# A search stage replanned: other costs and a port in the planner, low parts moved from GpSimd to VectorE, and the last two dense blocks of a chunk interleaved

## The chip, the cores and the metric

The kernel runs on one core of a Trainium2 chip. The metric is the device time of one execution in microseconds (us); the time given for a kernel is the median of several executions. Beside the times there is one execution recorded by the hardware profiler, and all rows below are from it. PE is TensorE (matmuls), PEld its weight loads, DVE is VectorE, ACT is ScalarE, POOL is GpSimd, SP is the engine that issues most DMAs.

## The reference, cut to what matters

One layer of a gated block on 4096 tokens of width 1024. The input is normalised and multiplied by one wide matrix; its columns become a sparse attention, a pooling branch and several gates.

```python
h = rms_norm(x, norm_g)
proj = h @ w_in
q, k, v, qi, ki, wi, z_a, u_b, z_b, gates = jnp.split(proj, SPLIT_POINTS, axis=-1)
...
logits = jnp.einsum('bqhd,bsd->bqhs', qib, ki)              # 8 index heads, width 32
iscore = jnp.einsum('bqhs,bqh->bqs', jax.nn.relu(logits), wib)
iscore = jnp.where(allowed[None], iscore, -jnp.inf)         # chunks of 64 keys
_, idx = lax.top_k(iscore, k_sel)                           # the best 256 keys of each query
...
outs.append((c - lagged) / count - ug[:, :, g])             # trailing means over 2, 4, 8, 16
mixed = jnp.einsum('bsgc,gcd->bsgd', pooled, pool_w)
b = mixed * pool_scale * silu(z_b)
g = sigmoid(gates + merge_bias)
y = g[:, :, 0] * (a @ w_branch_a) + g[:, :, 1] * (b @ w_branch_b)
x = x + y @ w_out
```

The search is the part from `logits` to `idx`: each query of a block of 128 needs the 256 best of all keys allowed to it. The dense projections are the columns `z_a`, `u_b`, `z_b` and `gates` of `h @ w_in`.

## The kernel before, in words

The work runs in stages. Phase 1 normalises x, computes the columns for attention and search, and writes the normalised input, transposed and split in a high and a low part, to DRAM. The index stage (`phase_index`, with `dense` in it) does the search for query blocks 2 to 31 and, beside it, the dense projections. Then come attention, the two branch products and the output product. Only the index stage is touched by the change.

**Split matmuls.** Products are computed as high x high + high x low + low x high. A weight tile is loaded (`wraw`), its high part `wgh` is a copy on ACT (L1157), and its low part `wgl` is the difference of the two, on POOL (L1158). Four of the 28 weight tiles are split earlier, in phase 1, on DVE (L697).

**Search.** For each block b there are 128(b+1) keys, in pieces of 1024. POOL fills the score tile with a tie-break by `iota` (L882). For each of 8 heads PE multiplies into one of two score banks `ps` (L894), ACT takes the Relu into one of four `rl` tiles (L897), and DVE multiplies by the head's weight and adds (L899, two SBUF inputs). The score tiles share one large tile, `ring`. Blocks form 18 groups, the large ones alone. For each group a threshold is found in seven rounds: ACT counts the scores over it by a Sign with a sum (L984), and some 20 small DVE instructions update it (`update`, L943 to L972). `finish` takes the largest of the rest (L1012, L1013), decides (L1020 to L1024, the last writes `flag`), and writes a bias row `bt` (L1032), which goes to DRAM.

**Dense.** Six sweeps of 5 or 4 channel tiles (blocks) go over 8 chunks of 512 tokens: 28 x 8 = 224 blocks. A chunk's h tiles (8 of them, 512 KB each) are loaded into a ring of 12. A block is 8 steps over the channel tiles k; a step is three matmuls of 512 columns into one of three banks `pd` (L1188 to L1190), and needs the pair of h tiles that holds channel tiles k and k+1. All steps stand in one chain. A finished block is read by ACT and DVE (`gate`, L1132 to L1139), or, for the first two blocks of four of the sweeps, by `pool`: ACT copies it (L1096, L1097), POOL adds shifted copies (`sums`, L1106), DVE takes the mean (L1115), ACT and POOL split it (L1117, L1118), PE multiplies it by the pool matrix (L393 to L395), and DVE scales it (L1122).

**What sets the order.** Nothing is scheduled on the chip: each engine runs its queue in the order in which the program was written, and waits at an instruction until its inputs and its tile are ready. That order comes from a planner, `Plan`. Each `pl.add` gives a step its engine, an estimated cost in us, a key, and the steps it follows. `Plan.run` simulates the engines: a free engine takes the ready step with the lowest key whose tiles are free in their rings, and the step's instructions are written out then. A dependent on another engine becomes ready 0.1 us (`LAT`) later, one on a DMA 2 us later. Search steps have keys from 12 to 1042, spread by a formula in `span`; a dense step's key is its place times `unit`; what follows a dense block has a very low key and so goes first.

```python
m = pl.add("pe", n * 0.42e-3, k_, mm, have + [base[o]] + ..., use=[ps, t])
r = pl.add("act", 0.05 + n * 0.834e-3, k_, ...activation(rl, ps, AF.Relu), [m], use=[ps, rl])
prev[o] = pl.add("dve", 0.1 + n * 1.04e-3, k_, ...scalar_tensor_tensor(acc, rl, wi, acc), [r, prev[o]], use=[rl])
...
prev = pl.add("pe", 5.0 / KT, t, mm, [l0, l1, have, prev], use=[pd, wh, wl, h0, h1])
t += unit / KT
```

Of the kernel before, what the change touches and what calls it, by code (L numbers as in the profile page):

```python
# [12 lines left out]
F32 = mybir.dt.float32  # L13
# [37 lines left out]
LAT = 0.1  # L51
# [73 lines left out]
class Step:  # L125
    def __init__(self, eng, cost, key, fn, after, use, form):
        self.eng, self.cost, self.key, self.fn, self.use, self.form = eng, cost, key, fn, use, form
        self.wait, self.then, self.ready = 0, [], 0.0
        for x in after:
            self.wait += 1  # L130
            x.then.append(self)
        for x in self.use:
            x.users += 1


class Plan:
# [11 lines left out]
    def new(self, name, role=None):  # L148
        return Tile_(name, role)
# [25 lines left out]
    def add(self, eng, cost, key, fn, after=(), new=(), use=(), form=0):  # L175
        s = Step(eng, cost, key, fn, [x for x in after if x is not None], (*new, *use), form)
        self.steps.append(s)
        return s

    def run(self, lat):  # L180
        ready = {}
        busy = {}
        form = {}
        now, order, done, left = 0.0, 0, [], len(self.steps)
        seq = {id(s): i for i, s in enumerate(self.steps)}

        def push(s):
            insort(ready.setdefault(s.eng, []), (s.key, seq[id(s)], s.ready))

        for s in self.steps:  # L190
            if not s.wait:
                push(s)
        while left:
            start, nxt = None, None
            for eng, q in ready.items():
                free = busy.get(eng, 0.0)
                if free > now:
                    nxt = free if nxt is None else min(nxt, free)
                    continue
                for i, (_, n, t) in enumerate(q):  # L200
                    if t > now:
                        nxt = t if nxt is None else min(nxt, t)
                        continue
                    s = self.steps[n]
                    if self.room(s.use):
                        start = (q, i, s)
                        break
                if start:
                    break
            if start:  # L210
                q, i, s = start
                del q[i]
                for x in s.use:
                    if x.t is None:
                        p = self.place(x.ring)
                        self.rings[x.ring][p] = x
                        x.t = self.make[x.ring](p)
                s.fn()
                s.end = busy[s.eng] = now + s.cost + (CHF if form.get(s.eng, 0) != s.form else 0.0)
                form[s.eng] = s.form  # L220
                heappush(done, (busy[s.eng], seq[id(s)]))
                continue
            if done and (nxt is None or done[0][0] <= nxt):
                now, n = heappop(done)
                s = self.steps[n]
                left -= 1
                for x in s.use:
                    x.users -= 1
                    if not x.users:
                        order += 1  # L230
                        x.freed = order
                for d in s.then:
                    d.wait -= 1
                    d.ready = max(d.ready, now + (2.0 if s.eng == "dma" else lat if d.eng != s.eng else 0.0))
# [20 lines left out]
class K:  # L255
# [520 lines left out]
    def phase_index(self):  # L776
# [92 lines left out]
        def scores(b, key, total, free):  # L869
# [6 lines left out]
            while os_:  # L876
# [3 lines left out]
                for o in some:  # L880
                    n = min(1024, L - o)
                    prev[o] = base[o] = pl.add("pool", 0.1 + n * 1.65e-3, key(0) - 3, lambda o=o, n=n: po.iota(  # L882
                        acc[:, o:o + n].bitcast(I32), pattern=[[1, n]], base=-(2 ** 31) + (27 << 23) + 1 + o,
                        channel_multiplier=0), free)
                for h in range(8):
                    for o in some:
# [4 lines left out]
                        def mm(ps=ps, o=o, n=n, h=h):  # L891
# [3 lines left out]
                        m = pl.add("pe", n * 0.42e-3, k_, mm, have + [base[o]] + kd[:max(0, (o + n - S) // P + 2)],  # L895
# [3 lines left out]
                        prev[o] = pl.add("dve", 0.1 + n * 1.04e-3, k_, lambda rl=rl, o=o, n=n, h=h: v.scalar_tensor_tensor(  # L899
                            acc[:, o:o + n], rl.t[:, :n], self.wi[:, b, h:h + 1], acc[:, o:o + n], op0=OP.mult,  # L900
                            op1=OP.add), [r, prev[o]], use=[rl])
# [3 lines left out]
        def topk(gi, key, scored):  # L905
# [68 lines left out]
            last = pl.add("dve", 1.0, key, start, [guessed], use=[tk])  # L974
            done = []
            for i in range(7):
# [13 lines left out]
                if i < 6:  # L990
                    last = pl.add("dve", 1.6 if i < 2 else 2.1, key, lambda i=i: update(i), ev, use=[tk])
            return done

        def finish(b, j, key, sg, tk, evals):
# [10 lines left out]
            s0 = pl.add("dve", 0.4, key, begin, evals, use=[tk, v9])  # L1005
            for p in range(n_p):
# [7 lines left out]
                pieces.append(pl.add("dve", 0.3 + n * 2.08e-3, key, best, [s0], use=[sg, z, v9, cand]))  # L1014
# [10 lines left out]
            s1 = pl.add("dve", 1.0, key, choose, pieces, use=[v9, cand, tk, sel, j9])  # L1025
            flags.append(s1)
            out = []
            for p in range(n_p):
# [3 lines left out]
                s = pl.add("dve", 0.08 + n * 0.52e-3, key, lambda bt=bt, o=o, n=n: v.tensor_scalar(  # L1032
# [33 lines left out]
        pl.run(LAT)  # L1066
# [5 lines left out]
    def dense(self, pl, new, rp):  # L1072
# [16 lines left out]
        def pool(c, g, t, pu, pz, done):  # L1089
# [11 lines left out]
            def sums():  # L1101
# [6 lines left out]
                if c == 0:  # L1108
                    po.tensor_tensor(cur[:, 16:32], cur[:, 16:32], self.cst[:, 32 + 16 * g:48 + 16 * g], op=OP.mult)
            s = chain[g] = pl.add("pool", 0.2 + 1.25 * (g + 1), k, sums, [e0, e1], use=[u, x0] + ([x1] if g else []))  # L1110
# [5 lines left out]
                cur.t[:, 16:], cur.t[:, 16:], 1.0 / win, u.t[:, 16:], op0=OP.mult, op1=OP.subtract), [s], use=[cur, u])  # L1116
# [3 lines left out]
            s = pl.add("pe", 0.62, k, lambda: self.mm3(pm.t, lambda k: wm[g][0], lambda k: wm[g][1],  # L1120
# [26 lines left out]
        def weight(s, m, kind, i, t):  # L1147
# [3 lines left out]
            def load():  # L1151
                o = 0
                for c0, w in cols[kind](i):
# [4 lines left out]
            l = pl.add("pool", 2.3, t - WSP, lambda: po.tensor_tensor(lo.t, raw.t, hi.t.bitcast(F32), op=OP.subtract),  # L1158
                       [h], use=[raw, hi, lo])
# [3 lines left out]
        unit = 5.04  # L1163
        prev = None
        for s, mine in enumerate(sweeps):
# [3 lines left out]
            for c in range(NCH):  # L1169
# [9 lines left out]
                for m, (kind, i) in enumerate(mine):  # L1179
                    pd = new("pd")  # L1180
                    wh, wl, have = W[s, m]
                    for k in range(KT):
                        (h0, l0), (h1, l1) = H[k // 2 * 2:k // 2 * 2 + 2]

                        def mm(k=k, pd=pd, wh=wh, wl=wl, h0=h0, h1=h1):
                            out = pd.t.rearrange("p (r n) -> p r n", n=P)
                            r1, r2 = h0.t[:, :, k % 2], h1.t[:, :, k % 2]
                            pe.matmul(out, wh.t[:, k], r1, start=(k == 0), stop=False)  # L1188
                            pe.matmul(out, wh.t[:, k], r2, start=False, stop=False)  # L1189
                            pe.matmul(out, wl.t[:, k], r1, start=False, stop=(k == KT - 1))  # L1190
                        prev = pl.add("pe", 5.0 / KT, t, mm, [l0, l1, have, prev], use=[pd, wh, wl, h0, h1])
                        t += unit / KT
# [1019 lines left out]
```

## Time and profile before

| | |
|---|---|
| median of 3 executions | 4097.2 us (4094.45 to 4098.45) |
| the profiled execution | 4089.81 us, its span 4088.1 us |
| PE / DVE / ACT / POOL busy in the span | 97% / 80% / 55% / 49% |
| mean granted TensorE clock | 0.990 |
| index stage | 418 to 2032 us |

A group of instructions is read as: line, engine, operation, out<-in by tile names, shapes, count | busy us, mean ns of one | idle time of the engine just before them, and what ended it. A matmul's record is longer than the distance to the next one. A row of waits gives the engine and line that waited, what released it, and the total, the number and the longest of the waits.

### The profile page before, as it was taken

The page shows a single profiled execution, that of the slowest core. Times are in us where ns is not written, and L with a number is a line of the kernel's source. Part 1 is how long each engine was busy: PE and PEld are TensorE (multiplying, and loading weights), DVE is VectorE, ACT ScalarE, POOL GpSimd, SP SyncE. Part 2 cuts the span into 40 slices and gives each one's busy share as a digit, 9 for nine tenths or more (in the row PEclk, how much of TensorE's full clock was granted, in tenths as well). Part 3 has the DMA queues.
Part 4 walks back from the last instruction along what each step waited for, and adds up shares of the span by engine and source line. Part 5 has one row for each costly group of instructions (what it writes and reads, how often), then busy time and mean ns, then how long its engine had stood idle before and what let it go on. Part 6 is the DMA issues. An engine that isn't in the chain of part 4 may idle for free. (4 is left out here: it accounts for less than half of the span.)

```text
span 4088.1 us, 63978 instructions
## 1 busy us (share of the span) xinstructions
PE 3964.7 (97%) x22958; PEld 3028.6 (74%) x22959; DVE 3255.0 (80%) x6399; ACT 2259.6 (55%) x3165; POOL 2021.8 (49%) x1616
## 2 busy tenths in 40 slices
PE   9999999999999999999889999999999999999999
PEld 8999887777777777888766666666666667887787
DVE  7555788888889888778689999999999995556654
ACT  5444787777767877877445555555454552111221
POOL 4554312122123223010028899999999994334653
PEclk9999999999999999999979999999999999999999
DMA  8877545445444455566554433333222215887543
GB/s 278 277 251 249 180 175 185 148 170 189 168 164 164 167 178 188 203 235 227 197 127 73 87 66 69 61 61 59 46 55 44 47 35 179 268 265 241 177 160 123
DMA packets 515986, 637.36 MB, mean 156 GB/s; under 512 B 230608, under 2 KB 365392, under 8 KB 511696
## 3 DMA queue, kind: packets, MB, share of 16 engines
q1 hardware_dynamic: 490576, 610.03, 47.4%
q10 hardware_dynamic: 25088, 23.21, 2.6%
q8 instruction: 181, 2.97, 0.3%
q14 instruction: 141, 1.16, 0.1%
HBM read 409.48 MB, written 191.76 MB: 147 GB/s over the span
## 5 line engine op out<-in xcount | busy, mean ns | idle before, releaser
L1656 POOL TENSOR_TENSOR acc<-acc,tt 128x1024 f32<-128x1024 f32 x388 | 927.6, 2391 | 62.2 <-ACT tt L1637 35.0
L1637 ACT ACTIVATE tt<-tt 128x1024 f32<-128x1024 f32 (+1 forms) x544 | 561.1, 1034 | 544.3 <-DVE tt L1638 513.5
L1189 PE MATMUL pd<-h,wgh 128*128 128x512 f32 x1792 | 705.6, 394 | 11.3 <-DMA h<-hD 11.2
L1188 PE MATMUL pd<-h,wgh 128*128 128x512 f32 x1792 | 710.8, 397 | 0.2 <-DMA h<-hD 0.2
L899 DVE SCALAR_TENSOR_TENSOR ring<-rl,wi,ring 128x1024 f32<-128x1024 f32 (+7 forms) x624 | 699.1, 1165 | 11.6 <-ACT rl L897 8.4
L1190 PE MATMUL pd<-h,wgl 128*128 128x512 f32 x1792 | 704.1, 393 | 0.0
L897 ACT ACTIVATE rl<-ps 128x1024 f32<-128x1024 f32 (+7 forms) x624 | 536.2, 887 | 184.7 <-DVE ring L899 67.5
L1638 DVE TENSOR_TENSOR tt<-st,bT 128x1024 f32<-128x1024 f32 (+1 forms) x504 | 600.5, 1193 | 12.0 <-PE st L1625 11.9
L984 ACT ACTIVATE sg<-ring,tk 128x2048 fp8e4<-128x2048 f32 (+9 forms) x322 | 485.2, 1508 | 63.8 <-DVE tk L972 34.1
L1677 PE MATMUL pv<-tt,vv 128*64 128x256 f32 x4224 | 515.2, 385 | 1.8 <-ACT ov L1698 1.4
L1566 DVE CUSTOM_DVE_ANT_1 jk<-ps,bias,mf 128x1024 bf16<-128x1024 f32 (+3 forms) x408 | 469.5, 1151 | 16.1 <-PE ps L1557 14.3
L1677 PEld LDWEIGHTS pv<-tt,vv 128*64 128x64 f32 x4224 | 285.6, 137 | 169.1 <-issue 34.8
L1189 PEld LDWEIGHTS pd<-h,wgh 128*128 128x128 f32 x1792 | 338.1, 189 | 85.3 <-DMA h<-hD 18.0
L1190 PEld LDWEIGHTS pd<-h,wgl 128*128 128x128 f32 x1792 | 337.6, 188 | 75.3
L1188 PEld LDWEIGHTS pd<-h,wgh 128*128 128x128 f32 x1792 | 337.7, 188 | 73.9 <-DMA h<-hD 0.6
L894 PE MATMUL ps<-kis,qT 128*128 128x512 f32 (+3 forms) x1136 | 344.1, 388 | 41.1 <-ACT rl L897 40.7
L1981 PE MATMUL p<-g,w 128*128 128x512 f32 x1488 | 345.5, 394 | 1.7 <-DVE g L1904 1.7
L1981 PEld LDWEIGHTS p<-g,w 128*128 128x128 f32 x1488 | 279.3, 188 | 67.7 <-DVE g L1904 2.1
L2130 PE MATMUL p<-w,g 128*128 128x512 f32 x1344 | 314.0, 396 | 3.8 <-DVE g L2109 2.1
L2130 PEld LDWEIGHTS p<-w,g 128*128 128x128 f32 x1344 | 253.5, 189 | 64.2 <-DVE g L2109 2.6
L1557 PE MATMUL ps<-kh,qh 64*128 64x512 f32 (+3 forms) x1320 | 264.6, 418 | 29.7 <-DVE mf L1566 26.8
L894 PEld LDWEIGHTS ps<-kis,qT 128*128 128x128 f32 x1136 | 206.8, 189 | 116.8 <-ACT rl L897 76.3
(360 smaller groups left out, 6737.4 us busy)
## 6 DMA issues: line engine op xcount, KB each, us to landing
h<-hD SPq DMA_DIRECT2D x384, 512.0 KB
g<-gD SPq DMA_DIRECT2D x80, 512.0 KB
hlD<-rhl SPq DMA_DIRECT2D x31, 1216.0 KB
gD<-sgm SPq DMA_DIRECT2D x128, 256.0 KB
q<-hlD SPq DMA_DIRECT2D x61, 512.0 KB
x<-x SPq DMA_DIRECT2D x32, 512.0 KB
hD<-hh SPq DMA_DIRECT2D x32, 512.0 KB
hD<-hl SPq DMA_DIRECT2D x32, 512.0 KB
```

Source lines behind the costliest of these rows:

```text
L894: pe.matmul(ps.t[:, s:e], t.t[:, h], self.kis[:, o + s:o + e], start=True, stop=True)
L897: r = pl.add("act", 0.05 + n * 0.834e-3, k_, lambda ps=ps, rl=rl, n=n: act.activation(rl.t[:, :n], ps.t[:, :n], AF.Relu), [m], use=[ps, rl])
L899: prev[o] = pl.add("dve", 0.1 + n * 1.04e-3, k_, lambda rl=rl, o=o, n=n, h=h: v.scalar_tensor_tensor(acc[:, o:o + n], rl.t[:, :n], self.wi ...
L1188: pe.matmul(out, wh.t[:, k], r1, start=(k == 0), stop=False)
L1189: pe.matmul(out, wh.t[:, k], r2, start=False, stop=False)
L1190: pe.matmul(out, wl.t[:, k], r1, start=False, stop=(k == KT - 1))
L1637: act.activation(tt.t[:, 0:n], tt.t[:, 0:n], AF.Exp)
L1638: ad = last_ve[0] = pl.add("dve", 0.07 + 0.54 * n, key, lambda: v.tensor_tensor(tt.t[:, 0:n], s.t[:, 0:n], bc(bt.t[:, 2 * p:2 * p + n, Non ...
L1656: gp.tensor_tensor(acc.t, first, tt.t, op=OP.add)
L1677: pe.matmul(pv.t[64 * f:64 * f + 64], vv[:, k, 64 * g:64 * g + 64], T[u, p].t[:, k % 2, 2 * f:2 * f + 2], start=(k == 0), stop=(k == b))
L1981: pe.matmul(p.t, blk[i].t[:, k, ms], two(x[k // 2][j].t, F32R)[:, k % 2], start=(k == i == j == 0), stop=(k == 3 and i == 1))
L2130: pe.matmul(p.t, quarter(Q.t, x, F32R)[:, k], blk[y].t[:, k], start=(fresh and k == x == y == 0), stop=(k == 3 and x == 1), skip_group_che ...
```

## The change

The planner: a step can have a number of parts that need the shared port (`port`). Such a step keeps its engine busy; its parts queue for one port, first come first served, DVE's and POOL's together. A DMA step is done, for its tiles and its dependents, `land` us after its cost; the index stage runs with 0.15 us between engines and 2.0 for `land`. The other stages call `run` as before.

```diff
+    def run(self, lat, land=0.0):
...
+                if s.port:
+                    busy[s.eng] = math.inf
+                    heappush(done, (now, seq[id(s)], s.port))
+                    continue
...
-                heappush(done, (busy[s.eng], seq[id(s)]))
+                heappush(done, (busy[s.eng] + (land if s.eng == "dma" else 0.0), seq[id(s)], 0))
...
+                if part:
+                    if part > 0:
+                        line.append((n, part))
+                    if line and shared <= now:
+                        n, part = line.pop(0)
+                        s = self.steps[n]
+                        shared = now + s.cost / s.port
+                        heappush(done, (shared, n, -1))
+                        heappush(done, (shared, n, part - 1))
+                        if part == 1:
+                            s.end = busy[s.eng] = shared
+                    continue
...
-        pl.run(LAT)
+        pl.run(0.15, 2.0)
```

The costs in the index stage (n is the piece's columns):

| step | before | after |
|---|---|---|
| iota, POOL | 0.1 + 1.65 n/1000 | 0.1 + 0.82 n/1000 |
| score matmuls, PE | 0.42 n/1000 | 0.452 n/1000 |
| score step, DVE | 0.1 + 1.04 n/1000 | 0.13 + 1.04 n/1000, port 1 |
| threshold start, DVE | 1.0 | 0.43, port 4 |
| update, DVE, rounds 0 and 1 / later | 1.6 / 2.1 | 1.75 / 2.18 |
| finish begin / best / choose, DVE | 0.4 / 0.3 + 2.08 n/1000 / 1.0 | 0.1 / the same, port 2 / 0.8, port 4 |
| bias row, DVE | 0.08 + 0.52 n/1000 | 0.13 + 0.52 n/1000 |
| sums, POOL, by group | 0.2 + 1.25 (g+1) | 1.45, 2.4, 3.7, 6.0, port g+2 |
| pooled mean, DVE | 0.67 | 0.67, port 1 |
| pool matmuls, PE | 0.62 | 0.68 |
| dense step, PE | 5.0/8 | 5.47/8 |

The program itself: two subtractions go from POOL to DVE, `unit` goes from 5.04 to 5.48, and the last two blocks of each chunk take turns by pairs of channel tiles.

```diff
-            s = pl.add("pool", 1.25, k, lambda: po.tensor_tensor(pq.t, cur.t[:, 16:], ph.t.bitcast(F32), op=OP.subtract),
-                       [s], use=[cur, ph, pq])
+            s = pl.add("dve", 0.6, k, lambda: v.tensor_tensor(pq.t, cur.t[:, 16:], ph.t.bitcast(F32), op=OP.subtract),
+                       [s], use=[cur, ph, pq], port=1)
...
-            l = pl.add("pool", 2.3, t - WSP, lambda: po.tensor_tensor(lo.t, raw.t, hi.t.bitcast(F32), op=OP.subtract),
-                       [h], use=[raw, hi, lo])
+            l = pl.add("dve", 1.19, t - WSP, lambda: v.tensor_tensor(lo.t, raw.t, hi.t.bitcast(F32), op=OP.subtract),
+                       [h], use=[raw, hi, lo], port=1)
...
-        unit = 5.04
+        unit = 5.48
...
-                for m, (kind, i) in enumerate(mine):
-                    pd = new("pd")
+                pds = [new("pd") for _ in mine]
+                todo = [(m, k) for m in range(len(mine) - 2) for k in range(KT)]
+                todo += [(m, k) for k0 in range(0, KT, 2) for m in (len(mine) - 2, len(mine) - 1) for k in (k0, k0 + 1)]
+                for m, k in todo:
+                    kind, i = mine[m]
+                    pd = pds[m]
...
-                        prev = pl.add("pe", 5.0 / KT, t, mm, [l0, l1, have, prev], use=[pd, wh, wl, h0, h1])
-                        t += unit / KT
+                    prev = pl.add("pe", 5.47 / KT, t, mm, [l0, l1, have, prev], use=[pd, wh, wl, h0, h1])
+                    t += unit / KT
+                    if k < KT - 1:
+                        continue
```

## Rows read from the trace of the kernel before

**Rows 1.** The page's first part: the span, and each engine's busy time, share of the span and instructions.
```profile
span 4088.1 us, 63978 instructions
...
PE 3964.7 (97%) x22958; PEld 3028.6 (74%) x22959; DVE 3255.0 (80%) x6399; ACT 2259.6 (55%) x3165; POOL 2021.8 (49%) x1616
```
**Rows 2.** The windows of the index stage, from its first dense matmul to its last: start:end, length, then busy time (and instructions) of PE, PEld, DVE, ACT and POOL, the granted clock, the share of the DMA engines and GB/s.
```profile
418.30:800.00 381.70, 371.91 (x1632) 299.03 (x1630) 311.16 (x775) 297.64 (x355) 84.33 (x92) 0.99 0.50 175
800.00:1400.00 600.00, 576.04 (x2507) 458.47 (x2507) 526.66 (x1377) 452.32 (x583) 157.53 (x142) 0.99 0.48 169
1400.00:1900.00 500.00, 484.77 (x2174) 387.72 (x2173) 394.97 (x1003) 397.44 (x545) 78.19 (x66) 1.00 0.59 201
1900.00:2032.50 132.50, 126.89 (x549) 101.14 (x547) 90.59 (x377) 75.94 (x150) 1.13 (x2) 0.99 0.59 203
sum 1614.20, PE 1559.61 PEld 1246.36 DVE 1323.38 ACT 1223.34 POOL 321.18; mean PE 389.90 PEld 311.59 DVE 330.84 ACT 305.83 POOL 80.29
```
**Rows 3.** The dense line L1188 over the stage (durations in ns: least/median/most, first and last start), and PE's timeline at the end of the stage: start, length, line, operation.
```profile
L1188 PE MATMUL pd<-h,wgh x1792: 387/389/628, 418.4 to 2031.7; 128*128 128x512 f32 x200
...
2032.12 0.40 PE L1190 MATMUL pd<-h,wgl 128*128 128x512 f32 x1
2034.13 0.85 PE L387 MATMUL st<-identr,k 128*128 128x128 f32 x8 [1.61 <-DVE zsm L1134]
```
**Rows 4.** PE's timeline in a stretch of dense matmuls only: the first and the 52nd of it, 51 issues apart.
```profile
2000.04 0.39 PE L1188 MATMUL pd<-h,wgh 128*128 128x512 f32 x1
...
2011.70 0.40 PE L1188 MATMUL pd<-h,wgh 128*128 128x512 f32 x1
```
**Rows 5.** Groups of instructions by line, PE: the other two dense lines, the scores, the search's transposes and one of the twelve kinds of pooling matmuls.
```profile
L1189 PE MATMUL pd<-h,wgh 128*128 128x512 f32 x1792 | 705.6, 394 | 11.3 <-DMA h<-hD 11.2
...
L1190 PE MATMUL pd<-h,wgl 128*128 128x512 f32 x1792 | 704.1, 393 | 0.0
...
L894 PE MATMUL ps<-kis,qT 128*128 128x512 f32 (+3 forms) x1136 | 344.1, 388 | 41.1 <-ACT rl L897 40.7
...
L387 PE MATMUL pt<-identr,q 128*128 128x128 f32 x240 | 28.1, 240 | 0.0
...
L394 PE MATMUL pd<-pl,wm3h 128*128 128x512 f32 x8 | 3.4, 422 | 0.8 <-POOL pl L1118 0.8
```
**Rows 6.** The waits of the index stage: who waited for whom, total us, times, longest.
```profile
PEld ps L894 <- ACT rl L897: 76.3, 105, 4.3
...
ACT rl L897 <- DVE ring L899: 67.5, 70, 5.2
...
ACT rl L897 <- PE ps L894: 62.0, 92, 3.2
...
ACT rl L897 <- DVE cand L1013: 47.6, 26, 5.5
...
PE ps L894 <- ACT rl L897: 40.7, 39, 3.9
...
DVE bt L1032 <- DMA biasD<-bt: 22.7, 15, 3.4
...
PEld pd L1189 <- DMA h<-hD: 18.0, 17, 2.6
...
PE pd L1189 <- DMA h<-hD: 11.2, 10, 2.2
...
PEld pd L394 <- POOL pl L1118: 3.9, 6, 1.2
```
**Rows 7.** Timelines of DVE, POOL and ACT between 1014 and 1033 us: a predicated copy beside POOL's adds, those adds, an update of the threshold from its first instruction (L943) to the score steps that follow it (L899), the same copy in it, and two Relus.
```profile
1014.80 1.01 DVE L951 COPY_PREDICATED tk<-mk,tk 128x4 f32<-128x4 int32 x1
...
1015.85 2.22 POOL L1106 TENSOR_TENSOR s<-s 128x525 f32<-128x525 f32 x2
...
1029.92 0.16 DVE L943 TENSOR_TENSOR tk<-tk 128x1 f32<-128x1 f32 x1 [0.53 <-ACT sg L984]
...
1030.71 0.18 DVE L951 COPY_PREDICATED tk<-mk,tk 128x4 f32<-128x4 int32 x1
...
1032.41 2.47 DVE L899 SCALAR_TENSOR_TENSOR ring<-rl,wi,ring 128x1024 f32<-128x1024 f32 x2
...
1030.36 1.92 ACT L897 ACTIVATE rl<-ps 128x1024 f32<-128x1024 f32 x2
```
**Rows 8.** Groups of instructions by line: the two subtractions on POOL, subtractions of the same shapes on DVE, and the predicated copy of single-block updates.
```profile
L1158 POOL TENSOR_TENSOR wgl<-wraw,wgh 128x1024 fp32r<-128x1024 f32 x24 | 65.2, 2716 | 133.1 <-ACT wgh L1157 116.5 <-DMA h<-hD 16.6
...
L1118 POOL TENSOR_TENSOR pl<-s,ph 128x512 fp32r<-128x512 f32 x32 | 47.7, 1491 | 31.3 <-ACT ph L1117 31.3
...
L697 DVE TENSOR_TENSOR wgl<-wraw,wgh 128x1024 fp32r<-128x1024 f32 x4 | 5.9, 1473 | 7.1 <-ACT wgh L693 7.1
...
L599 DVE TENSOR_TENSOR rhl<-row,rhl 128x512 fp32r<-128x512 f32 (+1 forms) x95 | 53.2, 590 | 53.4 <-ACT rhl L594 53.4
...
L951 DVE COPY_PREDICATED tk<-mk,tk 128x4 f32<-128x4 int32 x66 | 18.8, 285 | 0.0
```
**Rows 9.** The score step's line over the kernel (durations, first and last start), and the last `flag` on DVE's timeline.
```profile
L899 DVE SCALAR_TENSOR_TENSOR ring<-rl,wi,ring x624: 334/1275/3231, 439.1 to 1957.7; 128x1024 f32<-128x1024 f32 x130, 128x768 f32<-128x768 f32 x5, 128x512 f32<-128x512 f32 x5, 128x896 f32<-128x896 f32 x4
...
2023.18 0.16 DVE L1024 TENSOR_TENSOR flag<-sel 128x1 f32<-128x1 f32 x1
```

More of the change, by code (lines that the diff above doesn't have):

```diff
@@ L125, with __init__ @@
 class Step:
-    def __init__(self, eng, cost, key, fn, after, use, form):
-        self.eng, self.cost, self.key, self.fn, self.use, self.form = eng, cost, key, fn, use, form
+    def __init__(self, eng, cost, key, fn, after, use, form, port):
+        self.eng, self.cost, self.key, self.fn, self.use, self.form, self.port = eng, cost, key, fn, use, form, port
         self.wait, self.then, self.ready = 0, [], 0.0
@@ L173, in room, with add @@
             for (r, o), n in roles.items())
-    def add(self, eng, cost, key, fn, after=(), new=(), use=(), form=0):
-        s = Step(eng, cost, key, fn, [x for x in after if x is not None], (*new, *use), form)
+    def add(self, eng, cost, key, fn, after=(), new=(), use=(), form=0, port=0):
+        s = Step(eng, cost, key, fn, [x for x in after if x is not None], (*new, *use), form, port)
         self.steps.append(s)
         return s
-    def run(self, lat):
+    def run(self, lat, land=0.0):
         ready = {}
@@ L183, in run @@
         form = {}
-        now, order, done, left = 0.0, 0, [], len(self.steps)
+        now, order, done, left, shared, line = 0.0, 0, [], len(self.steps), 0.0, []
         seq = {id(s): i for i, s in enumerate(self.steps)}
@@ L233, in run @@
                     d.wait -= 1
-                    d.ready = max(d.ready, now + (2.0 if s.eng == "dma" else lat if d.eng != s.eng else 0.0))
+                    d.ready = max(d.ready, now + (2.0 if s.eng == "dma" and not land else lat if d.eng != s.eng else 0.0))
                     if not d.wait:
@@ L972, in update @@
                     v.copy_predicated(T, s1, lim[:, 0])
-            last = pl.add("dve", 1.0, key, start, [guessed], use=[tk])
+            last = pl.add("dve", 0.43, key, start, [guessed], use=[tk], port=4)
             done = []
@@ L990, in topk @@
                 if i < 6:
-                    last = pl.add("dve", 1.6 if i < 2 else 2.1, key, lambda i=i: update(i), ev, use=[tk])
+                    last = pl.add("dve", 1.75 if i < 2 else 2.18, key, lambda i=i: update(i), ev, use=[tk])
             return done
@@ L1004, in begin @@
                 v.tensor_copy(v9.t[:, 0:1], tk.t[:, 3, j:j + 1])
-            s0 = pl.add("dve", 0.4, key, begin, evals, use=[tk, v9])
+            s0 = pl.add("dve", 0.1, key, begin, evals, use=[tk, v9])
             for p in range(n_p):
@@ L1013, in best @@
                     v.max(v9.t[:, 1:9] if n_p == 1 else cand.t[:, p * 8:p * 8 + 8], z.t[:, :n])
-                pieces.append(pl.add("dve", 0.3 + n * 2.08e-3, key, best, [s0], use=[sg, z, v9, cand]))
+                pieces.append(pl.add("dve", 0.3 + n * 2.08e-3, key, best, [s0], use=[sg, z, v9, cand], port=2))
             def choose():
@@ L1024, in choose @@
                 v.tensor_tensor(self.flag[:, b:b + 1], sl[:, 1:2], sl[:, 2:3], op=OP.is_equal)
-            s1 = pl.add("dve", 1.0, key, choose, pieces, use=[v9, cand, tk, sel, j9])
+            s1 = pl.add("dve", 0.8, key, choose, pieces, use=[v9, cand, tk, sel, j9], port=4)
             flags.append(s1)
```

33 lines of the change are left out of this document (16 added, 17 removed).

## Prediction

> **What bounds the kernel now.** First the page's busy shares: PE 97% of the span, DVE 80%, ACT 55%, POOL 49% [rows 1]. That says PE, but it is a mean over stages, so the next view is the windows of the stage that the change touches, search with the dense projections: PE busy 1559.6 of 1614.2 us, DVE 1323.4, ACT 1223.3, POOL 321.2 [rows 2]. Its first dense matmul starts at 418.4, its last ends at 2032.5, and attention's first transposes follow 1.6 us later [rows 3]. Everything before and after is built by code that the diff leaves as it is, so the whole effect must lie in these 1614 us.
>
> A busy PE is not a PE at its rate. The records of a 512-column matmul are 390 ns long but overlap: in a stretch of dense blocks alone, 51 issues take from 2000.04 to 2011.70, 0.2286 us each [rows 4]. At that rate the stage needs: 3 x 1792 dense matmuls, 5376 x 0.2286 = 1229 us; scores, 8 heads x 128 x 525 (the sum of b+1 over blocks 2 to 31) = 537,600 columns, or 1050 times 512, 240 us; 4 groups x 8 chunks x 3 pooling matmuls, 22 us; 240 transposes of 128 columns, 14 us by the same rate (counts in [rows 5]). Sum 1505. So 109 us of the stage are lost on PE, although the busy column shows only 55 idle.
>
> The waits say where. PE and its weight loader wait for the Relu that frees a score bank, 76.3 + 40.7 = 117.0 us in 144 waits, for h tiles 18.0 + 11.2 = 29.2 us in 27, and 3.9 us for POOL's low part of the pooled tile [rows 6]. Each wait shows about 0.2 us more than it costs, because the loader runs ahead of the matmul; less that, some 88, 24 and 3 us. They sum to 115, so the 109 are explained within 6. The Relu itself waits for DVE (67.5 and 47.6) and for PE (62.0) [rows 6]: neither DVE nor PE is simply too slow. The order of each queue is written ahead by a planner that never lets PE wait for a bank while a dense step is ready; the waits are the distance between its costs and the chip's.
>
> **The change part by part.**
>
> *Costs in the plan.* A dense step of three matmuls goes from 5.0/8 = 0.625 to 5.47/8 = 0.684; the chip takes 3 x 0.2286 = 0.686. Scores go from 0.42 to 0.452 ns per column; the chip's is 0.446. So PE was planned 8% too fast and is now right. On DVE the 1024-wide score step goes from 1.165 to 1.195 planned; two back to back take 2.47 [rows 7], so 1.235. An update of the threshold goes from 2.1 to 2.18 planned, and takes 1029.92 to 1032.41, 2.49 [rows 7]. The port queue in the plan makes POOL's sums and DVE's two-input steps exclude each other. DMA buffers become free 2 us after the transfer rather than at its planned end, so that bt no longer looks free early (DVE waited 22.7 us for it [rows 6]).
>
> What stays unplanned: about 0.3 us in each of the later updates of large blocks (11 groups x 4, 14 us); the Relu's 0.96 (two take 1.92 [rows 7]) against 0.904 planned, on 416 large ones 23 us of ACT, which is off the path half the time; and POOL's sums blocking the updates. The last: a copy of four elements takes 0.18 us alone and 1.01 beside a POOL add [rows 7]; over its 66 uses it has a mean of 0.285 [rows 8], 7 us too much, and I double that for the rest of the update. The Trainium skill ("SBUF — State Buffer", Who interferes with whom) says a VectorE instruction with two SBUF inputs and a GpSimd one that reads SBUF exclude each other for the whole instruction. The trace agrees, 1.01 against 0.18. By that rule alone every POOL add could stand in front of an update to which the plan gives no port, and the time would be rival A's.
>
> I take 14 + 11 + 14 = 39 us of DVE and ACT time that the plan doesn't know, and, with a quarter more for what these rows don't show, 50 us of Relu waits left of 88: gain 38. Bounds: all 88 gone, or none. I choose near the middle because the PE error, the largest, is gone entirely, while DVE's is only halved.
>
> *Low parts on DVE.* POOL loses 24 weight low parts (65.2 us) and 32 pooled ones (47.7) [rows 8]. DVE gains 24 x 1.19 to 1.47 (its own four weight splits took 1.473) and 32 x 0.59 [rows 8]: 48 to 54 us. Of DVE's 1614 - 1323 = 291 idle us this takes a sixth. Relief: with POOL's 113 us go the waits that they lay on DVE, between 0 and 113 us. I take 30, about a quarter, nearer to none because POOL is busy in only a fifth of the stage; so DVE's net load is some +20 us; on the path nothing, as long as dense steps cover it, +54 if the cover goes. The 3 us of PE waiting on POOL goes.
>
> *Interleaving.* The last two blocks of a chunk use each pair of h tiles together, so the first pair comes free after 2.7 us of an 11 us stretch instead of 1.4 us of the last 5.5. With 12 h buffers and 8 in use, the next chunk's third pair may start loading 8.2 + 2.7 = 10.9 us before it is needed instead of 4.1 + 2.7 = 6.8. The 27 waits have a mean of 1.1 us [rows 6], less than the 4.1 gained: I leave 4 of 24 us, gain 20. Bounds: 24, or nothing if DMA bandwidth is short (its share is 0.48 to 0.59 [rows 2]: against). The number of matmuls doesn't change. Two of three pd banks are now held to a chunk's end; the third was drained 5 us earlier, so this costs nothing unless ACT is over 4 us late.
>
> *Keys.* A block's key step goes from 5.04 to 5.48, the search's keys (12 to 1042 by its formula) stay. Dense work keyed behind the search's end grows from 224 - 1042/5.04 = 17 blocks (95 us) to 34 (186 us). The last score step started at 1957.7, 75 us before the end [rows 9]. It should now lie 130 to 190 before. The search gets more of DVE while it runs: (1323 + 20 - 60 for gates in the longer tail) / (1556 - 170) = 93%, against (1323.4 - 90.6) / 1481.7 = 83% up to 1900 [rows 2].
>
> *Sum.* 38 + 20 + 3 = 61 off the stage, 1614 to 1553. The profiled execution took 4089.8, its span 4088.1 and 1.7 around it; 4090 - 61 = 4029. The median of the runs shown is 7.4 above that execution, so 4036, and I say 4040, the remainder for a restart of the clock at the new stage end (granted clock 0.99 in the stage [rows 2]).
>
> **Rivals.**
>
> A: the Relu waits only move. For: two engines out of five are still planned short, and 93% on DVE leaves little to absorb an error. Against: PE's 8% was the largest error. Then only the h waits go: 4097 - 20 = 4077 (4070 to 4088).
>
> B: the h gain is eaten by DVE's extra 20 net: 4097 +- 8. For: its low parts are two-input steps like the copy that POOL blocked [rows 7]. Against: 291 idle us on DVE.
>
> C: slower, because DVE becomes the bound of the search. Place: 800 to 1400, where DVE is busy 526.7 of 600 [rows 2], with the search now favoured and low parts ahead of its score steps by their keys. Price: with no relief the 54 us stand in front of score steps and return as Relu waits behind which dense matmuls queue on PE: 4097 + 54 - 20 = 4131; with half the relief 4106. It decides when the search is later than the dense blocks: its last flag is at 2023.2, only 9 us before the last dense matmul [rows 3, 9]. Against: the later dense keys give it 91 us of slack.
>
> D: the plan comes out nearly as the chip runs, with 20 us left: 4000.
>
> **How the numbers follow.** Forecast 4040, own range 4008 to 4070: 0.52. A 0.13, B 0.12, C 0.18, D 0.05. What a measurement can't tell from no change is about 0.2%, 8 us. Faster: 0.52 + 0.13 + 0.05 = 0.70; same 0.12; slower 0.18. The range goes from 4008, leaving D out, to 4110, which takes in A, B and the nearer half of C.
>
> **What would show it.** In the new windows the stage should be 1535 to 1575 long with DVE at 1320 to 1370 busy and POOL near 200; h waits under 8 us; Relu waits on PE near 50 to 80 as shown; 0.2286 per dense matmul unchanged. It is wrong if Relu waits are still above 100 (A), if DVE is over 90% busy and score steps end the stage (C), or if stretches outside 418 to 2032 change by more than 5 us.

## The result, and the profile after

The changed kernel takes 4060.3 us (median of 4 executions, 4056.34 to 4064.93) against 4095.8 for the kernel before (median of 4 that ran with it). The ratio is 0.9922, interval 0.9909 to 0.9934: 35 us less. It is faster, as forecast, but the forecast was 4040: 56 us were expected and 35 came.

The page of the profile after, its first part as in [rows 1]:

```profile
span 4063.2 us, 63923 instructions
...
PE 3971.9 (98%) x22958; PEld 3031.8 (75%) x22959; DVE 3226.9 (79%) x6455; ACT 2252.2 (55%) x3163; POOL 1925.7 (47%) x1560
```

DVE and POOL are both busy less, PE a little more: nothing here tells what happened. So to the stage's ends. The dense line L1209 and the score step L915 over the kernel (first and last start):

```profile
L1209 PE MATMUL pd<-h,wgl x1792: 387/389/628, 418.8 to 1989.2; 128*128 128x512 f32 x200
...
L915 DVE SCALAR_TENSOR_TENSOR ring<-rl,wi,ring x624: 279/1275/2305, 443.5 to 1938.2; 128x1024 f32<-128x1024 f32 x131, 128x896 f32<-128x896 f32 x4, 128x768 f32<-128x768 f32 x4, 128x512 f32<-128x512 f32 x4
```

The timeline at the stage's end, of PE, DVE (the last flag) and SP (the first load for attention):

```profile
1989.20 0.39 PE L1209 MATMUL pd<-h,wgl 128*128 128x512 f32 x1
...
1992.88 0.16 DVE L1040 TENSOR_TENSOR flag<-sel 128x1 f32<-128x1 f32 x1
...
1994.83 0.39 SPq L1375 DMA_DIRECT2D k<-hlD  x1
...
1998.93 1.23 PE L403 MATMUL st<-identr,k 128*128 128x128 f32 x8 [5.47 <-DMA k<-hlD]
```

The last dense matmul starts at 1989.2 instead of 2032.1 [rows 3]: the stage is 43 us shorter. But the last `flag` now comes 3.7 us after it, where it came 9 before [rows 9]. Here attention's loads are issued only after the flags are counted, so PE waits for them: 9.7 us from the last dense matmul to attention's first transposes, against 2.0 before [rows 3]. 7.7 us are given back there: 43 - 7.7 = 35.

The windows of the stage (as in [rows 2]), up to the dense end and up to the count of the flags:

```profile
418.30:1989.60 1571.30, 1555.30 (x6854) 1244.01 (x6852) 1295.54 (x3570) 1215.15 (x1626) 223.00 (x244) 1.00 0.55 188
418.30:1993.80 1575.50, 1555.56 (x6856) 1244.12 (x6854) 1299.54 (x3584) 1215.75 (x1627) 223.00 (x244) 1.00 0.55 188
```

DVE has 51 us of subtractions more than before and is still busy 24 us less (1323.4 to 1299.5), POOL 98 less. The stage's waits around PE, to be read beside [rows 6]:

```profile
ACT rl L913 <- PE ps L910: 84.2, 118, 3.9
...
PEld ps L910 <- ACT rl L913: 53.0, 124, 3.6
...
ACT rl L913 <- DVE ring L915: 26.8, 42, 2.0
...
ACT rl L913 <- DVE cand L1029: 13.2, 12, 2.4
PE ps L910 <- ACT rl L913: 13.1, 11, 3.2
...
PEld pd L410 <- DVE pl L1134: 2.0, 6, 0.7
...
PEld pd L1208 <- DMA h<-hD: 0.9, 1, 0.9
...
PE pd L1208 <- DMA h<-hD: 0.5, 1, 0.5
```

The h waits went from 30.0 (29.2 of them in [rows 6]) to 1.4 us, the Relu waits from 117.0 to 66.1. The Relu in turn waits less for DVE (26.8 for score steps instead of 67.5, 13.2 instead of 47.6 for the largest of the rest) and more for PE (84.2 instead of 62.0). The two subtractions as groups of DVE:

```profile
L1174 DVE TENSOR_TENSOR wgl<-wraw,wgh 128x1024 fp32r<-128x1024 f32 x24 | 29.1, 1218 | 4.1 <-ACT wgh L1173 4.0
...
L1134 DVE TENSOR_TENSOR pl<-s,ph 128x512 fp32r<-128x512 f32 x32 | 22.0, 687 | 16.8 <-ACT ph L1133 16.7
```

They take 51 us together, within the 48 to 54 that [rows 8] gave.

In the two profiled executions the spans differ by only 24.9 us (4088.1 and 4063.2). The rest is attention, whose code is the same: from its first transposes to its last sums it took 1381.9 us before and 1392.5 after. In the twelve other profiles of this study the same code took 1384.9 to 1391.8, and the changed kernel itself took 1386.8 the second time (e7), so these two are the ends of one spread.

### The profile page after: what moved, and what is told of

Read it like the earlier page. It is cut to its first block, busy times and chain, and to the rows that moved or that the text cites. A ratio compares the mean times of both kernels' runs of the same rounds, so it can differ in the third digit from the quotient of the medians.

```text
span 4063.2 us, 63923 instructions
## 1 busy us (share of the span) xinstructions
PE 3971.9 (98%) x22958; PEld 3031.8 (75%) x22959; DVE 3226.9 (79%) x6455; ACT 2252.2 (55%) x3163; POOL 1925.7 (47%) x1560
## 4 chain that ended last, share of the span: by engine, by line
PE 36%; DVE 7%; issue 4%; DMA 2%; SPq 1%; ACT 0%; POOL 0%; ACTq 0%; DVEq 0%
PE pv L1698 9%; PE st L1646 7%; PE p L2002 7%; PE p L2151 7%; DVE jk L1587 5%; PE ps L1578 4%; DVE tt L1659 1%; PE pt L1746 1%; DMA qm<-maxD 1%; PE pt L403 1%; PE st L1866 0%; PE st L403 0%; DMA g<-gD 0%; DVE mf L1587 0%; DMA yD<-g 0%
## 5 line engine op out<-in xcount | busy, mean ns | idle before, releaser
L1209 PE MATMUL pd<-h,wgl 128*128 128x512 f32 x1792 | 703.2, 392 | 0.0
L915 DVE SCALAR_TENSOR_TENSOR ring<-rl,wi,ring 128x1024 f32<-128x1024 f32 (+7 forms) x624 | 670.3, 1122 | 9.7 <-ACT rl L913 7.0
L913 ACT ACTIVATE rl<-ps 128x1024 f32<-128x1024 f32 (+7 forms) x624 | 533.3, 889 | 131.6 <-PE ps L910 84.2
L1000 ACT ACTIVATE sg<-ring,tk 128x2048 fp8e4<-128x2048 f32 (+8 forms) x322 | 485.3, 1509 | 83.3 <-DVE tk L988 25.9
L1209 PEld LDWEIGHTS pd<-h,wgl 128*128 128x128 f32 x1792 | 337.2, 188 | 75.7
L1118 POOL COPY halo<-u 128x16 f32<-128x16 f32 x32 | 12.7, 396 | 708.9 <-ACT u L1112 708.9
```

Source lines behind the costliest of these rows:

```text
L913: r = pl.add("act", 0.05 + n * 0.834e-3, k_, lambda ps=ps, rl=rl, n=n: act.activation(rl.t[:, :n], ps.t[:, :n], AF.Relu), [m], use=[ps, rl])
L915: prev[o] = pl.add("dve", 0.13 + n * 1.04e-3, k_, lambda rl=rl, o=o, n=n, h=h: v.scalar_tensor_tensor(acc[:, o:o + n], rl.t[:, :n], self.w ...
```

## The experiments

Each kernel's stage has two ends: the dense blocks' last matmul and the search's last flag. The table gives the start of both, the Relu waits of PE up to the dense end (the rows of PE and of its weight loader added, as in [rows 6]), the h waits in the same way, the start of attention's first transposes, and the median time. A ratio is to the kernel before on the same chip.

| kernel | last dense | last flag | Relu waits | h waits | attention | time | ratio (interval) |
|---|---|---|---|---|---|---|---|
| before | 2032.1 | 2023.2 | 117 | 30 | 2034.1 | 4095.8 | 1 |
| after | 1989.2 | 1992.9 | 66 | 1 | 1998.9 | 4060.3 | 0.9922 (0.9909, 0.9934) |
| e1 interleaving only | 2029.0 | 2048.5 | 119 | 0 | 2055.0 | 4117.2 | 1.006 (1.0042, 1.0078) |
| e2 no interleaving | 2021.5 | 1986.7 | 53 | 59 | 2023.1 | 4076.7 | 0.9961 (0.9949, 0.9973) |
| e3 low parts on POOL | 2009.5 | 2026.9 | 94 | 1 | 2032.5 | 4087.4 | 0.9991 (0.9981, 1.0001) |
| e4 no port in the plan | 1994.0 | 1923.7 | 72 | 0 | 1998.9 | 4057.8 | 0.992 (0.99, 0.994) |
| e9 program only | 1973.7 | 2019.0 | 47 | 0 | 2025.7 | 4085.6 | 0.9983 (0.9973, 0.9993) |
| e5 matmul costs of before | 1936.6 | 2084.8 | 29 | 0 | 2091.1 | 4148.2 | 1.0135 (1.0118, 1.0151) |
| e10 no landing time | 1993.5 | 1968.4 | 74 | 0 | 1999.0 | 4061.3 | 0.9927 (0.991, 0.9943) |
| e7 after, again | 1989.0 | 1992.7 | 64 | 1 | 1998.7 | 4059.6 | one run |
| e12 matmul costs and key step | 2087.8 | 1968.4 | 176 | 20 | 2089.8 | 4154.0 | 1.0152 (1.0135, 1.0169) |
| e11 balanced | 1987.0 | 1967.1 | 62 | 0 | 1992.2 | 4052.8 | 0.9899 (0.9882, 0.9915) |
| e13 other costs measured | 1984.5 | 1936.0 | 56 | 0 | 1989.1 | 4054.0 | 0.991 (0.9891, 0.9929) |
| e14 both | 1971.2 | 1957.9 | 36 | 0 | 1976.5 | 4038.3 | 0.986 (0.9842, 0.9878) |

In every row attention starts 1.6 to 6.7 us after the later of the two ends. Where the dense blocks are that end, it starts 1.6 to 2.0 us after them without the interleaving (before, e2, e12) and 4.6 to 5.5 with it (e4, e10, e11, e13, e14). Attention's first load stands on SP's queue behind the store of the second-last block's gate, and with the interleaving that block is finished just before the last one. These are the two on SP's timeline in before, 3.7 us ahead of the last dense matmul, and in e14, 0.4 us behind it:

```profile
2028.40 0.33 SPq L1136 DMA_DIRECT2D gD<-zsm  x1
2028.79 0.42 SPq L1354 DMA_DIRECT2D k<-hlD  x1
...
1971.62 0.32 SPq L1152 DMA_DIRECT2D gD<-zsm  x1
1972.04 0.37 SPq L1375 DMA_DIRECT2D k<-hlD  x1
```

So with an early flag, too, the changed kernel would have given back some 3 of the 7.7 us, by its interleaving; this is an estimate from these rows.

**The parts, one undone at a time.**

e1: before, with the loop of the change

```diff
+                todo = [(m, k) for m in range(len(mine) - 2) for k in range(KT)]
+                todo += [(m, k) for k0 in range(0, KT, 2) for m in (len(mine) - 2, len(mine) - 1) for k in (k0, k0 + 1)]
```

> The kernel before with nothing but the last two dense blocks of each chunk interleaved; old costs, low parts on GpSimd, old key step. Theory: the waits for h tiles come from the order of the dense steps, so they fall here from 29 us as shown (13 us of distance between matmuls, as the two timelines give it) to under 3 as shown, and the Relu waits stay near 117 as shown: 4095.8 - 12 = about 4084. Rival: the h waits went because the plan now books a transfer's landing, and then they stay near 29 as shown here and the time stays within 5 us of 4096.

e2: after, with the blocks one after the other

```diff
-                for m, k in todo:
+                for m, (kind, i) in enumerate(mine):
...
+                    for k in range(KT):
```

> The changed kernel with the dense blocks one after the other again, the rest as changed. Theory: h waits come back, 20 to 30 us as shown, about 13 us of stage: 4060 + 12 = about 4072, Relu waits near 66 as shown. Rival (the landing in the plan did it): h waits stay under 5 as shown and the time within 5 us of 4060.

The theory held for the cause of the waits in both: none with the interleaving, 59 us without it (twice what was expected), though the plan of e2 books the landing. These are two of e2's rows:

```profile
PEld pd L1205 <- DMA h<-hD: 30.8, 22, 4.0
PE pd L1205 <- DMA h<-hD: 22.7, 16, 3.6
```

The times did not follow. e1 is 25 us slower than before: the dense blocks end 3 us earlier, but the last flag 25 later, and attention waits for the flag. This was the first sight of the two ends. In e2 the dense end is the later one by 35, and undoing the interleaving costs 16.

e3: after, with both subtractions on POOL

```diff
-            s = pl.add("dve", 0.6, k, lambda: v.tensor_tensor(pq.t, ...
+            s = pl.add("pool", 1.25, k, lambda: po.tensor_tensor(pq.t, ...
...
-            l = pl.add("dve", 1.19, t - WSP, lambda: v.tensor_tensor(lo.t, ...
+            l = pl.add("pool", 2.3, t - WSP, lambda: po.tensor_tensor(lo.t, ...
```

> The changed kernel with the 24 weight low parts and 32 pooled low parts back on GpSimd at their old planned costs. Theory: the low parts cost DVE about as much as they free it of blocked steps, so within 10 us of 4060, with DVE's busy time in the stage 20 to 50 us lower in its own work and 10 to 40 higher in blocked steps. Rival 1 (the move is a main part of the gain): 4075 or more and Relu waits over 90 as shown. Rival 2 (DVE is the bound and the move costs): 4045 or less.

Rival 1 was right: 27 us slower. Undoing the move loses most of the change. (The two steps keep their `port=1`, so this plan also queues POOL's low parts for the port, which the plan of before did not.) Its window up to the count of the flags stands beside the one of after:

```profile
418.30:2027.80 1609.50, 1561.43 (x6858) 1247.91 (x6856) 1304.38 (x3530) 1215.25 (x1629) 325.52 (x300) 0.99 0.53 184
```

DVE is busy 1304.4 us here and 1299.5 in after, which has 51 us more to do on it. So the rest of DVE's work takes 56 us less with the move, more than the move costs. The largest part is the 624 score steps, whose mean falls from 1160 to 1122 ns, 24 us in all. The other 29 us by which the search ends earlier are idle time of DVE; in these two profiles 25 of them stand at one wait, that of L1138 for the pooling matmuls, which in e3 have their low part from POOL:

```profile
DVE zsm L1138 <- PE pd L411: 53.4, 19, 7.9
```

In after it is 28.7 us in 19 times. Between e1 and e9 the same move brought the flag 30 us forward and this wait stayed at 13, so this part has no settled cause.

e4: after, with the port queue of the planner off

```diff
-                if s.port:
+                if False and s.port:
```

> The changed kernel with the port queue of the planner switched off: the same costs, but POOL's sums and DVE's steps don't exclude each other in the plan. Theory (the matmul costs brought most of the fall of the Relu waits): Relu waits between 66 and 80 as shown, 4060 to 4070. Rival (the port brought it): Relu waits over 90 as shown, 4075 to 4090.

The waits fell in the theory's range, the time 2 us below it: the port queue brings nothing. That the matmul costs brought the fall doesn't follow from this, and e5 speaks against it. But the queue shifts the ends: without it the flag is 69 us earlier and the dense end 5 later.

e9: before, with the interleaving and the low parts on DVE, and nothing else of the change

```diff
+            s = pl.add("dve", 0.6, k, lambda: v.tensor_tensor(pq.t, ...
...
+            l = pl.add("dve", 1.19, t - WSP, lambda: v.tensor_tensor(lo.t, ...
```

> The kernel before with the two changes of the program, low parts on VectorE and the last two blocks interleaved, but all costs, the key step and the planner as before (and the moved steps at 1.19 and 0.6). Theory, from the four runs so far (two ends, the dense blocks' and the search's last flag, and the later one counts): the interleaving brings the dense end to about 2029 in the old plan, and the low parts bring the flag from 2048 to about 2015, so the dense blocks decide: 4085 to 4092. Then the new costs are worth the other 25 to 30 us. Rival (the program is all of it): 4055 to 4067.

The time was within the theory, for the wrong reason. The dense blocks end at 1973.7, earlier than in after, with only 47 us of Relu waits; it is the search that ends late:

```profile
PEld ps L894 <- ACT rl L897: 36.1, 70, 3.0
...
PE ps L894 <- ACT rl L897: 10.7, 14, 2.6
```

So PE's waits fall without any of the new costs.

**What the matmul costs do.**

e5: after, with the matmul costs of before (and 0.62 for the pool matmuls)

```diff
-                    prev = pl.add("pe", 5.47 / KT, t, mm, [l0, l1, have, prev], use=[pd, wh, wl, h0, h1])
+                    prev = pl.add("pe", 5.0 / KT, t, mm, [l0, l1, have, prev], use=[pd, wh, wl, h0, h1])
...
-                        m = pl.add("pe", n * 0.452e-3, k_, mm, ...
+                        m = pl.add("pe", n * 0.42e-3, k_, mm, ...
```

> The changed kernel with the matmul costs of before (dense step 5.0/8, scores 0.42 ns per column, pool matmuls 0.62) and all else as changed. Theory (matmuls planned 8% too fast were the main part of the Relu waits): Relu waits 90 or more as shown, dense end at 2010 or later, 4075 to 4090. Rival (the matmul costs hardly matter, the DVE costs or the landing do): Relu waits under 75 as shown and within 6 us of 4060.

e12: before, with the matmul costs and the key step of after

> The kernel before with only the matmul costs of the change in its plan (dense step 5.47/8, scores 0.452 ns per column, pool matmuls 0.68) and the key step 5.48; program, other costs and planner as before. Theory (two ends: a matmul that the plan books longer leaves room for fewer dense steps between score steps, so the search ends earlier, the dense blocks later, and PE waits more for the Relu): last flag 1925 to 1965, dense end 2060 to 2090, Relu waits over 140 as shown, so slower: 4120 to 4150. Rival (right costs bring fewer waits, as forecast): Relu waits under 90 as shown, dense end at 2010 or earlier, 4065 to 4085.

e5 refuted both views: with matmuls planned 8% too fast PE waits less, 29 us, the dense end is 53 us earlier and the flag 92 later. From it came the theory of e12, which holds in direction: right matmul costs with the new key step make the kernel 61 us slower, with 176 us of Relu waits, though the flag (1968.4) came 3 us later and the time 4 us longer than the ranges given. How much of this the key step does isn't shown; in e5 it stays at 5.48, so there the matmul costs alone move the ends. PE's waits of e12:

```profile
PEld ps L894 <- ACT rl L897: 121.7, 191, 5.3
...
PE ps L894 <- ACT rl L897: 54.5, 62, 4.8
```

In its own time the planner doesn't let PE idle while a dense step is ready. A matmul booked shorter lets it put more dense steps between two score steps. On the chip these take longer than booked, so the score bank is free long before its turn: PE doesn't wait, and the search runs late. Booked right, fewer dense steps stand between; every delay of DVE or ACT that isn't booked then shows as a wait of PE, and the search runs early. The order on PE's timeline shows the mixing: ahead of the 568th of the 1136 score matmuls stand 2559 dense ones before and 2295 in e12, 2538 after and 2892 in e5. What it does to the waits is argued from the two runs.

e10: after, with `pl.run(LAT)`

> The changed kernel with the planner's latency 0.1 and no landing time of DMAs, as before. Theory (the interleaving alone keeps the h tiles early): h waits under 5 us as shown, within 8 us of 4060. Rival (the landing helps too): h waits over 10 us as shown or more waits of DVE for bt, 4070 or more.

The theory held: neither the landing time nor the longer latency is needed for the time. The landing was to keep bt from looking free early, but DVE's wait for it didn't fall with the change: 22.7 us before, 24.1 after, 33.2 in e10.

e7: after, a second time

> The changed kernel once more, for its second profile. In the first the stage was 43 us shorter but the span only 25: 7.7 us were lost where attention starts (its first loads are issued after the last flag, which came 3.3 us after the last dense matmul instead of 9 before), and 10.6 between attention's first transposes and its last sums. Theory: the first loss is in the program's order and comes again, 6 to 10 us from the last dense matmul's start to attention's first transposes plus the time of before; the second is one execution's chance: 1375 to 1390 here instead of 1392.5, and the span about 4055. Rival: 1390 or more again, so attention is made slower by how it starts.

The theory held: 9.7 us from the last dense matmul to attention again, 1386.8 for attention, and a span of 4057.8.

**A version that beats both.** If the two ends trade, the best plan lets both fall together, the flag some 10 us first.

e11: e4, with

```diff
-                    prev = pl.add("pe", 5.47 / KT, t, mm, [l0, l1, have, prev], use=[pd, wh, wl, h0, h1])
+                    prev = pl.add("pe", 5.27 / KT, t, mm, [l0, l1, have, prev], use=[pd, wh, wl, h0, h1])
...
-                        m = pl.add("pe", n * 0.452e-3, k_, mm, ...
+                        m = pl.add("pe", n * 0.438e-3, k_, mm, ...
```

> The changed kernel with the port queue off in the plan and the matmul costs 43% of the way back to those of before (dense step 5.27/8, scores 0.438). Without the port the last flag came at 1924 and the dense end at 1994, so the search has 70 us to spare. From the changed kernel to the one with the old matmul costs the flag moved +92 and the dense end -53. Theory (the two ends trade): flag about 1963, dense end about 1971, Relu waits 50 to 60 as shown, 4030 to 4042. Rival (PE's waits can't be traded, they are the plan's errors elsewhere): dense end within 8 us of 1994 and 4052 or more.

Both conditions of the rival are met, each by 1 us: the dense end moved by 7 us and not 23, and the time is 4052.8. The flag moved as the theory said (1967).

e13: e4, with the costs that the prediction had named as short

```diff
+                        r = pl.add("act", 0.095 + n * 0.844e-3, k_, ...
+                        prev[o] = pl.add("dve", 0.17 + n * 1.04e-3, k_, ...
...
+                    last = pl.add("dve", (1.75 if i < 2 else 2.27) + 0.22 * (n_e > 1), key, ...
```

> The changed kernel with the port queue off and the steps that the prediction named as planned too short set to what the trace of before shows: Relu 0.96 for 1024 columns, score step 1.235, later updates of large blocks 2.49. Matmul costs as in the change. Theory A (two ends trade, and a cost that is right in its place also removes waits): flag 1945 to 1985, dense end 1968 to 1982, Relu waits under 55 as shown, 4030 to 4046, below the 4052.8 of the balanced kernel. Theory B (only the ratio of planned matmul to planned search time counts, wherever it is put): a point on the same curve as the balanced kernel: dense end 1983 to 1990, 4048 to 4058.

Flag, dense end, waits and time all miss A's ranges, and dense end and time lie in B's. Against e4 the dense end came 9.5 us earlier for a flag 12 later, and the Relu waits fell from 72 to 56. What B doesn't say is that the flag is 49 us ahead of the dense end here and 20 in e11, at the same time.

e14: e13, with 5.32 for the dense step and 0.442 for the scores

> The kernel with the measured Relu, score step and update costs and the port off, with the matmul costs a third of the way back (dense step 5.32/8, scores 0.442). It has 49 us between flag (1936) and dense end (1985) to trade. By the balanced kernel's step (flag +43, dense -7 for 43%) theory B gives flag about 1968 and dense about 1980, 4046 to 4052. Theory A, by the step from the changed kernel to the one with old matmul costs (flag +92, dense -53 for 100%), gives flag 1966, dense 1967 and 4034 to 4042.

4038.3 us, A's range, ratio 0.986: 22 us below the changed kernel. The flag is at 1957.9, 13 us before the last dense matmul, and PE waits least of all kernels whose flag comes first. Its window up to the dense end:

```profile
418.30:1971.60 1553.30, 1544.38 (x6859) 1245.72 (x6857) 1306.71 (x3585) 1217.64 (x1628) 223.28 (x244) 1.00 0.55 190
```

Its Relu waits of PE:

```profile
PEld ps L910 <- ACT rl L913: 30.3, 74, 2.2
...
PE ps L910 <- ACT rl L913: 5.4, 8, 1.8
```

And PE's timeline at the handover, where PE waits for attention's first load, which the flag no longer holds back:

```profile
1971.21 0.39 PE L1209 MATMUL pd<-h,wgl 128*128 128x512 f32 x1
1976.52 0.72 PE L403 MATMUL st<-identr,k 128*128 128x128 f32 x4 [4.92 <-DMA k<-hlD]
```

Why e14 followed A's step of the dense end (-13 us for a third) and e11 did not (-7 for 43%) is open.

## Why the prediction was right or wrong

**Where the time is.** Right: all of it is in the index stage and its handover to attention. Stretches behind differ by the spread of attention alone. The prediction's sign of being wrong, more than 5 us there, came up in the first profile (10.6) and just not in the second (4.9); the spread is wider than it allowed.

**What PE loses, and the price of a wait.** Here the sizes failed. The prediction took 0.2 us off each wait and came to 88 + 24 + 3 us for 109 lost. Adding 76.3 and 40.7 counts the same time twice: all 39 of PE's waits lie inside waits of its loader, as in these two rows of before, where the scores come 1.27 us late and 2.66 are added up:

```profile
699.87 0.30 PEld L894 LDWEIGHTS ps<-kis,qT 128*128 128x128 f32 x2 [1.54 <-ACT rl L897]
699.87 0.50 PE L894 MATMUL ps<-kis,qT 128*128 128x512 f32 x1 [1.12 <-ACT rl L897]
```

The distances between matmuls on PE's timeline, less 0.2286 us for 512 columns, show it better. Before, 109 us were lost: 51 before scores that waited for a Relu, 14 for h tiles, 3 for POOL, and 41 in small lengthenings, nearly all with no wait. After, 66: 23, 1 and none, with 42 of the rest. So the 109 was right and its agreement with the sum of the waits was chance: over a third of it belongs to none of these waits, and a Relu wait costs less than half of what the two rows show together. Some of the rest follows from waits all the same: the 17 us of the stage at half the granted clock cost about 7 us. One such stretch is 709.40 to 716.20, granted clock 0.50, after PE had waited 3.20 us:

```profile
708.60 0.72 PE L894 MATMUL ps<-kis,qT 128*128 128x512 f32 x2 [3.20 <-ACT rl L897]
...
713.31 0.63 PE L1188 MATMUL pd<-h,wgh 128*128 128x512 f32 x1
713.74 0.63 PE L1189 MATMUL pd<-h,wgh 128*128 128x512 f32 x1
```

**The Relu waits, gain 38.** The sum's term was close (measured 28), the mechanism was wrong, so this closeness is luck. "The PE error, the largest, is gone entirely" was to lower them. e5 and e12 show the opposite: with the old matmul costs they fall to 29, and right matmul costs, with the key step, raise them to 176 and cost 61 us. What lowers them in both plans is the move of the low parts from POOL (e3 to after: 94 to 66; e1 to e9: 119 to 47). What brought the first 23 of the 51, from 117 to e3's 94, wasn't separated.

**Low parts on DVE, +20 us of load.** The own cost was right (51, 48 to 54 forecast), the relief was mis-sized: 56 us (e3 against after), not 30, within its bounds of 0 and 113. DVE's load falls instead of rising. This move, priced at nothing on the path, is worth 27 us of the 35 when it alone is undone. The Trainium skill ("SBUF — State Buffer", Who interferes with whom), with its exclusive lock for the whole instruction, speaks for such a relief; the runs agree: 56 us less on DVE's other steps for 115 us that POOL's two subtractions take in e3. Which steps were blocked wasn't counted.

**Interleaving, gain 20.** Right in mechanism: the waits go from 30 to 1 with it and return to 59 without it. As a part of the stage it was 13, of which some 3 are lost again at the handover where the dense blocks end last; undone in the new plan it costs 16; alone in the old plan it made the kernel slower by 25, as the search then ends 25 us later; why the old plan puts the search off wasn't separated.

**Keys.** Wrong. The last score step was to lie 130 to 190 us before the dense end; it lies 51 before (1938.2). DVE was to be 93% busy up to there and was 83% (1256.1 of 1519.9 us). The 93 is reckoned with a stage of 1556 us where the sum gives 1553, which changes nothing. What the key step does alone isn't shown, as no run changes nothing else; what the runs do show is that the search follows how much dense work the plan puts between its steps.

**Rival C** named the right place for the wrong reason: the search does become the later end, by 3.7 us, and 7.7 are lost at the handover. Its point of decision, flag against last dense matmul, is the one that says in every row of the table when attention starts. e1 and e5 have C's end without its cause: in e1 the low parts are still on POOL, and e5 has them on DVE as after has. C's price for half the relief, 4106, doesn't come out of its terms: half of the 54 us gives 4104, half of the 30 taken as relief 4116.

**The sum.** 61 off the stage were forecast and 43 came (28 + 13 + 3, less 1 for the rest), then 7.7 were lost at the handover, for which the sum had no term. It had 4 us for a restart of the clock: at attention's start the granted clock is 0.50 for 41.0 us before and 51.2 after, 6.7 of these before attention begins, so attention has only 3.5 us more of it. 4040 missed by 20, inside the range.

## What to carry to other kernels

Where two streams share engines in an order written ahead, look at both ends of the stage, not at the waits: the later end counts, and a stretch with few waits may only mean that the other stream is late. Booked costs are first of all the ratio at which the streams are mixed; a cost that becomes right on one side alone can cost more than it gives, here 61 us together with the key step. Undo each part alone before believing a sum: interleaving (16), low parts (27) and all of costs, keys and planner (25, e9) make 68 us for a change of 35, because each of them moves both ends, by different amounts (the low parts by 20 and 34 us), and only the later one counts.

## What the runs showed of the hardware

A subtraction of 128x1024 that takes POOL 2.72 us in the mean [rows 8] takes DVE 1.22, and with the two subtractions off POOL DVE's other steps took 56 us less (e3 against after), the score step 1122 instead of 1160 ns in the mean. The predicated copy's mean, 0.285 us before [rows 8] and 0.231 after, is no sign of it: in e3, with the subtractions on POOL, it is 0.228. After a wait of PE of 3.20 us the granted clock was 0.50 for 6.8 us, and the next dense matmuls came every 0.43 us instead of 0.23. Attention's same instructions took between 1381.9 and 1392.5 us in fourteen profiles, so a single pair of spans can be off by 10 us on a change of 35.
